# Low parts of weight tiles: two ScalarE copies and an adding DMA in place of a VectorE subtraction

## The chip, the core and the metric

The kernel runs on one core of a Trainium2 chip. The core has a tensor engine (TensorE, PE in the profile; its weight loads are PEld), a vector engine (VectorE, DVE), a scalar engine (ScalarE, ACT), GpSimd (POOL) and SyncE (SP). Each has a queue of its own and works it off in order; they meet through semaphores. DMA transfers are issued from a queue (SP's, or POOL's) and carried by 16 DMA engines that all queues share. The metric is the device time of one execution in microseconds.

## What is computed

One decoder layer on 1024 tokens of width 1024, all in float32. The reference, cut to what matters:

```python
for l in range(DEPTH):                                          # DEPTH = 1
    h = _layer_norm(ALPHA * h + 0.5 * _swiglu(h, ffn1...), ln1_g[l], ln1_b[l])
    mix = _token_mixers(h, w_in[l], lower_bounds[l], ..., w_out[l])
    h = _layer_norm(ALPHA * h + mix, ln2_g[l], ln2_b[l])
    xa = _memory_cross_attention(h, mem, mem_ln_g[l], mem_ln_b[l], xa_w_q[l], xa_w_k[l],
                                 xa_w_v[l], xa_w_o[l])
    h = _layer_norm(ALPHA * h + xa, ln3_g[l], ln3_b[l])
    h = _layer_norm(ALPHA * h + 0.5 * _swiglu(h, ffn2...), ln4_g[l], ln4_b[l])
```

The token mixers multiply h by `w_in` (1024 x 3072), whose column blocks feed a gated recurrence of four heads and a spatial gating unit; both outputs side by side are multiplied by `w_out` (1024 x 1024). The attention multiplies by `xa_w_q` and, at its end, by `xa_w_o` (1024 x 1024 each).

## The kernel before

Every product of two float32 matrices is made as three products in a shorter format (`F32R`): an operand is split into a high part, its value rounded to that format, and a low part, the rest. `mm3` (L130) then issues high x high, high x low and low x high (L131 to L133), all into the same PSUM bank.

Weights come in tiles of 128 partitions x 1024 values, 512 KB. `load_raw` (L112) issues the load on SP's queue (L118) into one of three buffers with the tag `raw`. `split_w` (L121) takes one of six `whi` and one of five `wlo` buffers and calls `split` (L108): ScalarE copies the raw tile into the high part (L109), VectorE subtracts the high part from the raw tile into the low part (L110). `load_split` (L127) is both. A raw buffer is free again when the low part has read it; high and low buffers are free again when TensorE has issued the last product that reads them.

The stages follow one another on TensorE: keys and values of the memory, the first FFN, the token mixers, the output projection, the attention, the second FFN. The FFNs have helpers of their own for their weights (`w_combos`, `down`), which call `split_w` directly. In the other stages weights are used in three ways:

- `feat_group` (L138), called by `feat_unit` (mixers: forget gate `wf`, query `wq`, gating input `wu`) and by `q_proj` (attention, `waq`): one tile holds all 1024 rows of 128 columns; 24 products with it make one bank.
- `token_units` (L779): four tiles hold 1024 rows of 512 columns and stay for four units, one per token tile, of 24 products each (values `wiv`, gating values `wvs`, output gate `wg`). They take four of the five low buffers as long as they are used.
- `down_group` (L226), for `w_out` (`wd_mx`) and `xa_w_o` (`wd_xa`): a group of two or three token tiles keeps two banks each; every step k loads one tile and issues 6 products with it per token tile. The groups are (0, 1), (2, 3, 4) and (5, 6, 7), and each loads all eight tiles anew.

The mixers go by halves of the tokens: values (`wiv`), gates and queries by head, gating inputs, gating values (`wvs`) of the first half; then the values and first gate of the second half; then the output gate (`wg`) of the first half; then the rest of the second half. The first group of `w_out` comes after the gating values of the second half, then the output gate of the second half, then the two groups of three. In the attention the products of the first group of `xa_w_o` lie between those of the heads.

What follows a product on other engines (recurrence, norms, gates) runs as coroutines: `tick` (L73) counts the time of issued products, and a coroutine yields how much of it should be issued before it goes on. `residual_norm` (L214) yields at least 6 us before its transposes. The norms use POOL for the reciprocal root, two instructions each (`rsqrt_eps`, L176; L179, L181, L182).

The program is issued in this order to a planner that simulates the engines and chooses each engine's final order from its own estimates of durations, so an instruction may move past others of its queue. POOL issues no DMA before the change. Six PSUM banks of 128 x 512 are shared by the products (`ps_mm`), two more by the transposes (`ps_tr`).

Of the kernel before, what the change touches and what calls it, by code (L numbers as in the profile page):

```python
# [8 lines left out]
F32 = mybir.dt.float32  # L9
F32R = mybir.dt.float32r  # L10
# [5 lines left out]
P = 128  # L16
# [17 lines left out]
def hybrid_layer_kernel(ctx: ExitStack, tc: tile.TileContext, a, out):  # L34
# [29 lines left out]
    # Work that follows a matrix product on other engines runs as a coroutine: where the tensor  # L64
    # engine would wait for it, it yields the time of other products (in us) to issue first.
# [26 lines left out]
    # the tensor engine's clock rises while it works: transposes until the first tile is there  # L92
# [9 lines left out]
    # left and right operands of the products of the FFNs' down projection, by pair of feature tiles  # L102
# [26 lines left out]

    def mm3(ps, lh, ll, rh, rl, first, last):  # L130
        nc.tensor.matmul(ps, lh, rh, start=first, stop=False)  # L131
        nc.tensor.matmul(ps, lh, rl, start=False, stop=False)  # L132
        nc.tensor.matmul(ps, ll, rh, start=False, stop=last)  # L133
# [11 lines left out]
    def to_xT(h_tile, tt, ks, name, keep=None):  # L145
        """Transpose the 128-column blocks of a token-major tile into xT's k-tiles ks; with keep,
        also as they are into tiles by (half of k, half of the tokens, pair of k-tiles)."""
        for _ in to_xT_steps(h_tile, tt, ks, name, keep):
            pass
# [57 lines left out]
    def layer_norm(y, gb, bb, name):  # L207
        """y: [P, 1024] tile, normalized over its free dim in place."""
# [5 lines left out]
    def residual_norm(tt, lag, acc, res_src, gb, bb, dst, name, keep=None):  # L214
        """dst = LN(alpha * res_src + acc) for a token tile, and its transpose."""
# [10 lines left out]
    def down_group(w, nk, grp, operand, res_src, gb, bb, dst, name, keep=None):  # L226
        """dst = LN(alpha * res_src + operand^T @ w) for the token tiles of grp; yields after each k."""
        acc = {tt: [ps_mm(f"acc_{name}_{tt}_{dh}") for dh in range(2)] for tt in grp}
        for k in range(nk):
            wh, wl = load_split(w[k * P:(k + 1) * P, :], f"wd_{name}_{grp[0]}_{k}")  # L230
# [21 lines left out]
    # Winograd's form of Strassen's product for W^T X^T with 2x2 blocks: rows are two feature  # L252
    # tiles, the contraction and the tokens are halved.
    def x_combos(xf, name):
        """Right operands of the products, in two stages."""
# [22 lines left out]
    def w_combos(w, f1, f2, name, pool=None):  # L278
        """Left operands of the products, in two stages: those of the first part, then all."""
# [19 lines left out]
    def strassen(wc, rhs, name):  # L299
        """Products of two feature tiles with all tokens, a tile each, in two parts: the first  # L300
        multiplies blocks of X as they are."""
# [26 lines left out]
    def ffn(wg, wu, wd, g, b, res_src, dst, make_xT, xf, name, start=None):  # L328
        """start: products that come before, given what to do late in them; without it, the first pair of
        feature tiles is multiplied without Strassen's form."""  # L330
# [70 lines left out]
    # The down projection h W has its blocks by half of the tokens, parity of the feature tile and  # L401
    # half of the columns.
    SLOT = {1: 0, 5: 1, 6: 2, 2: 3, 4: 4, 7: 5, 3: 6}

    def store_h(kp, h, tmp):
        """Left operands of the seven products for the feature tiles 2 kp and 2 kp + 1."""
# [10 lines left out]
    def down(wd, res_src, gb, bb, dst, make_xT, name):  # L417
# [5 lines left out]
        def right(ps, k, n):  # L423
            """Right operands: of two products for pair k, or of one for n pairs from k;
            combinations for later ones are kept."""
# [33 lines left out]
        # operands are made some steps ahead of their products  # L459
# [8 lines left out]
        # of product 3, the first operands take the place of xT, which has been used by then  # L468
# [22 lines left out]
        def pair(ps, when):  # L491
            """Two products, all tiles in step; returns their banks."""
# [20 lines left out]
        def single(p, done, hold):  # L513
            """One product; in its last steps, as many as hold says, its tiles end one after the other."""
# [36 lines left out]
        def norm(tt, wait):  # L551
# [3 lines left out]
            if tt < 4:  # L555
                # xT's place is free: what the scalar engine writes there is not used
# [222 lines left out]
    def token_units(half, c0, name, evac):  # L779
        """One unit per token tile of the half: x[tile] @ w_in[:, c0:c0+512], then evac(i, psum)."""  # L780
        wts = []

        def unit(i):
            if not wts:
                wts.extend(load_split(w_in[2 * j * P:(2 * j + 2) * P, c0:c0 + 512]
# [12 lines left out]
    def feat_unit(half, c, name, evac):  # L798
        """The feature tile c of x @ w_in for the half, transposed."""
        evac(feat_group(load_split(wcol(w_in, c), f"{name}{half}"), half, f"ps_{name}{half}"))  # L800

    class Mixers:
        """What the mixers keep of one half: v, o and u in pairs of tiles, and by head [k | q] and
        [b | log f, then scores]."""
# [80 lines left out]
        def recurrence(self, h):  # L885
            """Head h: gated scores within chunks of 128, states between the chunks, normed output."""
# [12 lines left out]
            def prep(j):  # L899
                """Levels 2j and 2j+1: k and q scaled by their decay to the border between their  # L900
                blocks; the last pair holds level 6 and k's decay to the end of its chunk."""
# [57 lines left out]
            # exp(b_end), exp(b) q  # L959
# [109 lines left out]
    qs, prs = {}, {}  # L1069

    def q_proj(half, c):
        wt = load_split(wcol(a["xa_w_q"][0], c), f"waq{half}_{c}")
# [134 lines left out]
```

## Time and profile before

| | us |
|---|---|
| median of 2 runs | 2037.99 |
| the two runs | 2035.06 and 2040.92 |
| span of the profiled execution | 2032.8 |

The span is the time from the first to the last instruction of one profiled execution; what lies around it is not in the profile. No other time of that execution is recorded, so the span is compared with the median of the runs, which is 5.2 us longer.

Where the stages lie in the span, by the first and the last product of each group on TensorE:

| stage | tile | from (us) | to (us) |
|---|---|---|---|
| mixers, values of both halves | `ps_wiv` | 704.5 | 877.6 |
| mixers, gating values of both halves | `ps_wvs` | 813.2 | 1019.9 |
| mixers, output gate of both halves | `ps_wg` | 893.3 | 1082.7 |
| output projection | `acc_mx` | 1022.2 | 1152.6 |
| attention, queries | `paq` | 1152.8 | 1265.6 |
| attention, output projection | `acc_xa` | 1275.2 | 1386.2 |

How to read the lines that follow: "L110 DVE ... x24 | 28.9, 1219 | 6.4 <-PE ..." is a group of instructions of line 110 on VectorE that ran 24 times, was busy 28.9 us in all and 1219 ns on average, and before which the engine had been idle for 6.4 us, ended by what stands behind the arrow. Names are those of the tiles: `_r` is a raw tile, `_h` a high part, `_l` a low part. A row of DMA issues ends with the KB of one transfer and the median time from its issue to its landing. In a table of stretches, a row has the stretch, its length, the busy time of each engine in it with the count of instructions, the clock that TensorE was granted, the busy share of the 16 DMA engines and the rate.

### The profile page before, as it was taken

The page shows a single profiled execution, that of the slowest core. Times are in us where ns is not written, and L with a number is a line of the kernel's source. Part 1 is how long each engine was busy: PE and PEld are TensorE (multiplying, and loading weights), DVE is VectorE, ACT ScalarE, POOL GpSimd, SP SyncE. Part 2 cuts the span into 40 slices and gives each one's busy share as a digit, 9 for nine tenths or more (in the row PEclk, how much of TensorE's full clock was granted, in tenths as well). Part 3 has the DMA queues.
Part 4 walks back from the last instruction along what each step waited for, and adds up shares of the span by engine and source line. Part 5 has one row for each costly group of instructions (what it writes and reads, how often), then busy time and mean ns, then how long its engine had stood idle before and what let it go on. Part 6 is the DMA issues. An engine that isn't in the chain of part 4 may idle for free.

```text
span 2032.8 us, 25339 instructions
## 1 busy us (share of the span) xinstructions
PE 2015.5 (99%) x9646; PEld 1689.1 (83%) x9646; DVE 1504.1 (74%) x2246; ACT 890.0 (44%) x1239; POOL 102.5 (5%) x144
## 2 busy tenths in 40 slices
PE   8999999999999999999999999999999999999998
PEld 7888888888888888888888888888888888888886
DVE  5987677677668967948796855678776776776688
ACT  6633333334533467547644344444333333344432
POOL 0000000000002010100110100010000000000021
PEclk8999999999999999999999999999999999999999
DMA  8333233237887632123156522353232332378874
GB/s 263 122 114 119 78 114 119 78 119 250 290 289 261 222 116 73 53 63 105 41 176 228 162 88 74 122 197 119 88 126 82 104 127 81 109 249 291 297 254 172
DMA packets 244250, 306.88 MB, mean 151 GB/s; under 512 B 14368, under 2 KB 154272, under 8 KB 244128
## 3 DMA queue, kind: packets, MB, share of 16 engines
q1 hardware_dynamic: 244128, 305.26, 45.3%
q8 instruction: 76, 1.25, 0.2%
q14 instruction: 46, 0.38, 0.1%
HBM read 234.44 MB, written 70.78 MB: 150 GB/s over the span
## 4 chain that ended last, share of the span: by engine, by line
PE 93%; DVE 3%; DMA 2%; POOL 1%; issue 1%; SPq 0%; ACT 0%; POOLq 0%; DVEq 0%; ACTq 0%
PE st_gf L131 7%; PE st_uf L131 7%; PE st_gf L133 7%; PE st_uf L133 7%; PE st_gf L132 7%; PE st_uf L132 7%; PE dp_f L133 6%; PE dp_f L131 6%; PE dp_f L132 6%; PE psl L939 2%; PE acc_xa L131 1%; PE acc_xa L133 1%; PE acc_xa L132 1%; PE paq L131 1%; PE paq L133 1%; PE paq L132 1%
## 5 line engine op out<-in xcount | busy, mean ns | idle before, releaser
L132 PE MATMUL dp_f<-wd_f_l,ah_f 128*128 128x512 f32 x552 | 213.3, 390 | 0.0
L131 PE MATMUL dp_f<-wd_f_h,ah_f 128*128 128x512 f32 x552 | 208.4, 390 | 0.0
L133 PE MATMUL dp_f<-wd_f_h,al_f 128*128 128x512 f32 x552 | 206.1, 390 | 0.1
L133 PEld LDWEIGHTS dp_f<-wd_f_h,al_f 128*128 128x128 f32 x552 | 103.7, 188 | 22.2 <-DVE al_f L110 0.9
L132 PEld LDWEIGHTS dp_f<-wd_f_l,ah_f 128*128 128x128 f32 x552 | 103.6, 188 | 21.6
L131 PEld LDWEIGHTS dp_f<-wd_f_h,ah_f 128*128 128x128 f32 x552 | 103.6, 188 | 21.2
L109 ACT ACTIVATE wd_f_h<-wd_f_r 128x1024 fp32r<-128x1024 f32 x72 | 73.2, 1022 | 97.7 <-DVE wd_f_r L436 28.3
L110 DVE TENSOR_TENSOR al_f<-ar_f,ah_f 128x1024 fp32r<-128x1024 f32 x72 | 84.5, 1174 | 24.5 <-ACT ah_f L109 23.6
L109 ACT ACTIVATE ah_f<-ar_f 128x1024 fp32r<-128x1024 f32 x72 | 73.3, 1019 | 59.2 <-DMA ar_f<-lops 54.3
L110 DVE TENSOR_TENSOR wd_f_l<-wd_f_r,wd_f_h 128x1024 fp32r<-128x1024 f32 x72 | 84.3, 1175 | 12.5 <-ACT wd_f_h L109 12.2
L316 DVE TENSOR_TENSOR top_uf<-bot_uf,st_uf 128x512 f32<-128x512 f32 x21 | 14.4, 686 | 81.8 <-PE st_uf L133 81.8
L315 ACT ACTIVATE bot_gf<-st_gf 128x512 f32<-128x512 f32 x21 | 12.5, 597 | 137.1 <-PE st_gf L133 137.1
L560 POOL TENSOR_SCALAR nm_f<-nm_f 128x1 f32<-128x1 f32 x8 | 10.7, 1336 | 1198.8 <-ACT xl L559 1198.8
L131 PE MATMUL st_gf<-xh,wg_f_h 128*128 128x512 f32 x168 | 65.4, 389 | 0.0
L133 PE MATMUL st_gf<-xh,wg_f_l 128*128 128x512 f32 x168 | 65.4, 389 | 0.0
L131 PE MATMUL st_uf<-xh,wu_f_h 128*128 128x512 f32 x168 | 65.4, 389 | 0.0
L132 PE MATMUL st_uf<-xl,wu_f_h 128*128 128x512 f32 x168 | 65.4, 389 | 0.0
L133 PE MATMUL st_uf<-xh,wu_f_l 128*128 128x512 f32 x168 | 65.4, 389 | 0.0
L132 PE MATMUL st_gf<-xl,wg_f_h 128*128 128x512 f32 x168 | 65.3, 389 | 0.0
L109 ACT ACTIVATE wg_f_h<-wg_f_r 128x1024 fp32r<-128x1024 f32 x44 | 46.4, 1056 | 36.2 <-PE st_gf L132 29.3
L109 ACT ACTIVATE wu_f_h<-wu_f_r 128x1024 fp32r<-128x1024 f32 x44 | 46.3, 1053 | 35.7 <-issue 27.2
L110 DVE TENSOR_TENSOR wu_f_l<-wu_f_r,wu_f_h 128x1024 fp32r<-128x1024 f32 x44 | 53.6, 1219 | 3.2 <-PE acc_xa L132 3.2
(456 smaller groups left out, 5960.1 us busy)
## 6 DMA issues: line engine op xcount, KB each, us to landing
ar_f<-lops SPq DMA_DIRECT2D x66, 512.0 KB, 5.0
wd_f_r<-in_ffn_w_down_dram SPq DMA_DIRECT2D x56, 512.0 KB, 4.8
wg_f_r<-in_ffn_w_gate_dram SPq DMA_DIRECT2D x44, 512.0 KB, 3.8
wu_f_r<-in_ffn_w_up_dram SPq DMA_DIRECT2D x44, 512.0 KB, 3.8
wd_mx_r<-in_w_out_dram SPq DMA_DIRECT2D x24, 512.0 KB, 3.6
wd_xa_r<-in_xa_w_o_dram SPq DMA_DIRECT2D x24, 512.0 KB, 3.5
lops<-bot_gf SPq DMA_DIRECT2D x21, 512.0 KB, 2.7
lops<-top_uf SPq DMA_DIRECT2D x21, 512.0 KB, 2.8
```

Source lines behind the costliest of these rows:

```text
L109: order(nc.scalar.activation(hi, src, AF.Copy))
L110: order(nc.vector.tensor_tensor(lo, src, hi.bitcast(F32), op=ALU.subtract))
L131: nc.tensor.matmul(ps, lh, rh, start=first, stop=False)
L132: nc.tensor.matmul(ps, lh, rl, start=False, stop=False)
L133: nc.tensor.matmul(ps, ll, rh, start=False, stop=last)
L315: nc.scalar.activation(b0, product(1), AF.Copy)
L316: nc.vector.tensor_tensor(t0, b0, product(2), op=ALU.add)
L560: nc.gpsimd.tensor_scalar(nmean, nmean, -1.0 / D, None, op0=ALU.mult)
L939: nc.tensor.matmul(psl[:m, (i * NC2 + c) * 64:(i * NC2 + c + 1) * 64] .rearrange("p (n b) -> p n b", b=B), e[:, :m], blk(e, B)[:, :, 1, :] ...
```

## The change

A new helper, `load_parts`, takes the place of `load_split` in `down_group`, `token_units`, `feat_unit` and `q_proj`. ScalarE writes the high part as before. It then writes the negated high part into the low buffer, and a DMA from POOL's queue adds the raw tile to it in SBUF. The helpers of the FFNs and the keys and values of the memory still use `split`. The comments taken out elsewhere change nothing.

```diff
+    def load_parts(view, name):
+
+        raw = load_raw(view, name)
+        hi = wpool.tile(list(raw.shape), F32R, tag="whi", bufs=6, name=f"{name}_h")
+        lo = wpool.tile(list(raw.shape), F32R, tag="wlo", bufs=5, name=f"{name}_l")
+        nc.scalar.activation(hi, raw, AF.Copy)
+        nc.scalar.activation(lo, hi.bitcast(F32), AF.Copy, scale=-1.0)
+        nc.gpsimd.dma_start(lo, raw, accum_op=ALU.add)
+        return hi, lo
...
         for k in range(nk):
-            wh, wl = load_split(w[k * P:(k + 1) * P, :], f"wd_{name}_{grp[0]}_{k}")
+            wh, wl = load_parts(w[k * P:(k + 1) * P, :], f"wd_{name}_{grp[0]}_{k}")
...
             if not wts:
-                wts.extend(load_split(w_in[2 * j * P:(2 * j + 2) * P, c0:c0 + 512]
+                wts.extend(load_parts(w_in[2 * j * P:(2 * j + 2) * P, c0:c0 + 512]
                                       .rearrange("(k p) c -> p k c", p=P), f"{name}{half}{j}")
                            for j in range(KT // 2))
...
-        evac(feat_group(load_split(wcol(w_in, c), f"{name}{half}"), half, f"ps_{name}{half}"))
+
+        evac(feat_group(load_parts(wcol(w_in, c), f"{name}{half}"), half, f"ps_{name}{half}"))
...
     def q_proj(half, c):
-        wt = load_split(wcol(a["xa_w_q"][0], c), f"waq{half}_{c}")
+        wt = load_parts(wcol(a["xa_w_q"][0], c), f"waq{half}_{c}")
```

## The prediction

> **What bounds the kernel now.** I read the page first: the busy shares, then the chain that ended last.
>
> ```profile
> span 2032.8 us, 25339 instructions
> ...
> PE 2015.5 (99%) x9646; PEld 1689.1 (83%) x9646; DVE 1504.1 (74%) x2246; ACT 890.0 (44%) x1239; POOL 102.5 (5%) x144
> ...
> q1 hardware_dynamic: 244128, 305.26, 45.3%
> ...
> PE 93%; DVE 3%; DMA 2%; POOL 1%; issue 1%; SPq 0%; ACT 0%; POOLq 0%; DVEq 0%; ACTq 0%
> ```
>
> TensorE is busy for 2015.5 of 2032.8 us, so at most 17.3 us of the span can be won by making any other engine faster. The next view is the table of stretches, to see where these 17.3 us lie (columns: PE, PEld, DVE, ACT, POOL busy with counts, clock, DMA share, GB/s).
>
> ```profile
> 0.00:60.00 60.00, 51.95 (x345) 48.06 (x346) 36.42 (x60) 36.55 (x79) 3.32 (x16) 0.91 0.90 277
> ...
> 740.00:800.00 60.00, 60.00 (x327) 50.97 (x325) 41.90 (x96) 44.91 (x54) 2.80 (x5) 1.00 0.27 82
> ...
> 1020.00:1060.00 40.00, 39.58 (x238) 34.32 (x236) 37.20 (x89) 19.35 (x27) 3.62 (x6) 1.00 0.57 196
> ...
> 1900.00:2033.00 133.00, 124.01 (x545) 101.62 (x543) 105.74 (x123) 45.34 (x54) 19.80 (x20) 0.98 0.67 230
> ```
>
> The start loses 8.05 us, the end 8.99 us; neither is touched. Of what is left, 0.42 us stands at 1020 to 1060, where VectorE is busy for 37.2 of 40 us. So the changed stages (mixers, output projection, attention) have half a microsecond to win. How fast TensorE eats weights, I take from the timeline:
>
> ```profile
> 1117.65 0.39 PE L132 MATMUL acc_mx<-wd_mx_l,xh 128*128 128x512 f32 x1
> ...
> 1119.92 0.39 PE L133 MATMUL acc_mx<-wd_mx_h,xl 128*128 128x512 f32 x1
> ```
>
> Ten products lie between these two starts, 0.227 us each (the 0.39 of one row overlaps its neighbours). A weight tile of 512 KB feeds 24 products in the mixers and the queries, 5.45 us; 18 in a group of three token tiles, 4.09 us; 12 in a group of two, 2.72 us.
>
> **The change, part by part.** VectorE loses one subtraction per tile.
>
> ```profile
> L110 DVE TENSOR_TENSOR wd_xa_l<-wd_xa_r,wd_xa_h 128x1024 fp32r<-128x1024 f32 x24 | 29.3, 1222 | 25.5 <-PE paq L133 16.9 <-PE acc_xa L132 7.8 <-issue 0.3
> L110 DVE TENSOR_TENSOR wd_mx_l<-wd_mx_r,wd_mx_h 128x1024 fp32r<-128x1024 f32 x24 | 28.9, 1219 | 6.4 <-PE acc_mx L132 4.2 <-issue 1.7 <-ACT wd_mx_h L109 0.2
> ...
> L110 DVE TENSOR_TENSOR waq_l<-waq_r,waq_h 128x1024 fp32r<-128x1024 f32 x16 | 19.6, 1224 | 27.8 <-PE paq L133 22.7 <-PE acc_mx L132 2.6 <-issue 2.5
> ...
> L110 DVE TENSOR_TENSOR wg_l<-wg_r,wg_h 128x1024 fp32r<-128x1024 f32 x8 | 9.8, 1224 | 6.6 <-ACT wg_h L109 3.2 <-PE ps_wf L133 3.0 <-PE ps_wiv L132 0.2
> ...
> L110 DVE TENSOR_TENSOR wiv_l<-wiv_r,wiv_h 128x1024 fp32r<-128x1024 f32 x8 | 9.6, 1218 | 0.0
> ```
>
> With 8 each of the six kinds from w_in (first and last shown) that is 24 + 24 + 16 + 48 = 112 tiles, 112 x 1.22 = 137 us of VectorE removed. TensorE did not wait for it: worth 0 to 0.4 us, I take 0.
>
> *ScalarE* gains one 128x1024 copy per tile, 112 x 1.06 = 119 us by the row of the high part:
>
> ```profile
> L109 ACT ACTIVATE wd_mx_h<-wd_mx_r 128x1024 fp32r<-128x1024 f32 x24 | 25.4, 1059 | 27.0 <-DMA wd_mx_r<-in_w_out_dram 12.2 <-PE acc_mx L133 10.7 <-PE ps_wvs L133 2.3
> ...
> DVE waq_l L110 <- PE paq L133: 22.7, 9, 4.1
> ```
>
> The tightest place is 740 to 800: 44.91 us busy, and TensorE can eat at most 60 / 5.45 = 11 tiles there, so ScalarE ends at 56.6 of 60. The cover is its remaining idle time; without it a bank's evacuation comes 1 to 4 us later. The wait for a free low-part buffer, until now VectorE's (up to 4.1 us), now stands in ScalarE's queue, with the evacuation of the products behind it. Six PSUM banks at 5.45 us a unit hide that: 0, and 2 x 1.06 us per unit at the worst if no bank were spare.
>
> *The accumulating DMA*, 112 of 512 KB, is the unknown; the trace has no DMA from POOL and none that adds. Call L its time from issue to landing. Nearest rows:
>
> ```profile
> wd_mx_r<-in_w_out_dram SPq DMA_DIRECT2D x24, 512.0 KB, 3.6
> ...
> lops<-bot_gf SPq DMA_DIRECT2D x21, 512.0 KB, 2.7
> ...
> kv<-kv SPq DMA_DIRECT2D x4, 512.0 KB, 6.8
> ...
> r_mx<-res SPq DMA_DIRECT2D x8, 512.0 KB, 8.4
> ```
>
> Lower bound: one plain transfer out of SBUF, 2.7 us. Upper: the slowest plain one and another after it, 8.4 + 2.7 = 11.1. I take 5.0 where the queues are quiet: 2.7, plus a second read of 512 KB at the rate of q1 (45.3% of 2032.8 us for 305.26 MB, 1.58 us), plus 0.7 for POOL's part, as its small instructions take (below). Where the queues are crowded, kv took 6.8 against 3.6; half of that surcharge makes L = 7, nearer to the quiet rows because these stretches are crowded only in part. The Trainium skill, page "DMA: Bandwidth & Descriptors", section "Anatomy of one DMA — SWDGE (gpsimd) path", gives about 2.0 us plus bytes over 436 GB/s for a plain DMA from this queue, 3.2 us here (an estimate from that page; no run here shows it); by it no term below is left and the time would be 2038.
>
> A tile's low part used to be ready 1.22 us after the high part; now after 1.06 + L and two hand-overs. What this can hold up is the buffers: three raw, six high, five low.
>
> ```profile
> SPq L118 <- DVE wd_mx_l L110: 98.9, 19, 28.2
> ...
> 1097.62 0.33 SPq L118 DMA_DIRECT2D wd_mx_r<-in_w_out_dram  x1
> ...
> 1096.36 1.23 DVE L110 TENSOR_TENSOR wd_mx_l<-wd_mx_r,wd_mx_h 128x1024 fp32r<-128x1024 f32 x1 [0.19 <-ACT wd_mx_h L109]
> ...
> L110 DVE TENSOR_TENSOR wd_mx_l<-wd_mx_r,wd_mx_h x24: 1171/1220/1234, 988.6 to 1131.6; 128x1024 fp32r<-128x1024 f32 x24
> ...
> L132 PE MATMUL acc_mx<-wd_mx_l,xh x128: 387/389/476, 1022.6 to 1152.4; 128*128 128x512 f32 x128
> ...
> L220 DVE SCALAR_TENSOR_TENSOR r_mx<-r_mx,acc_mx x16: 669/680/681, 1051.2 to 1155.2; 128x512 f32<-128x512 f32 x16
> ```
>
> Loads wait on SP until the low part has read a raw buffer. One turn of a raw buffer is issue 0.3, load 3.6, two copies 2.12, two hand-overs of 0.2, and L: 6.42 + L for three tiles. At L = 5 that is 3.8 us a tile (before: 2.1), below 5.45 and 4.09, so mixers, queries and groups of three keep their pace; they also have a lead, the last low part of w_out being done at 1133 and last used at 1152.
>
> Two places are short.
> - The seams, where a set of four column blocks (products of token tiles) ends and the next tiles follow at once: value-gate to wiv of the second half, value-gate to w_out. There a low buffer comes free 5.45 us before it is wanted, and 1.06 + 0.4 + 5.0 = 6.46 are needed: 1.0 us each, 2.0 together (0 at L = 2.7, 14 at 11.1).
> - The first group of w_out (two token tiles) with the gate's four tiles after it. The group runs from 1022.6 to 1051.2, with recurrences between, and all four gate tiles are wanted within 5.45 us after it: 12 tiles, three loaded beforehand, in 34 us. This stretch is crowded, so L = 7 and 4.47 us a tile: 9 x 4.47 = 40.2, 6 us late (0 at L = 2.7; 9 x 5.84 = 52.6, 18 late at 11.1). The same group of the attention runs between heads, with time to spare.
>
> *Queues that are passed.* On POOL the DMA waits for ScalarE's copy, and behind it stand the small steps of the norms:
>
> ```profile
> L179 POOL TENSOR_SCALAR ve_xa<-mv_xa 128x1 f32<-128x1 f32 x8 | 8.1, 1013 | 216.7 <-DVE mv_xa L196 216.7
> ...
> L182 POOL TENSOR_TENSOR rs_mx<-ve_mx,mhalf 128x1 f32<-128x1 f32 x8 | 6.4, 802 | 0.7
> ```
>
> VectorE waits for them, then the transposes. Their cover is the 6 us and more of products that the code puts before each transpose: 0; without it some 2 us for each of 16 norms. On SP, stores and residual loads stand behind a load that now waits longer; their users are covered in the same way.
>
> The sum: 2.0 + 6 = 8 us onto the profiled span, 2032.8 to about 2041. The median of the runs shown, 2037.99, is 5.2 us over that span; I keep this difference: 2046 us.
>
> **The rivals.**
>
> *Hidden altogether, 2037.* L near 3 and VectorE's relief at 1020 to 1060 pays its 0.4 us. For it: TensorE's idle time is nowhere in these stages. Against it: the raw buffers' turn grows in any case. This is also the time if the change works without doing anything for the clock.
>
> *The DMA engines become the bound in the output projection, 2072.*
>
> ```profile
> 1022.00:1051.00 29.00, 29.00 (x166) 24.75 (x165) 26.20 (x69) 13.27 (x15) 1.88 (x2) 1.00 0.60 205
> 1051.00:1087.00 36.00, 35.58 (x204) 30.80 (x203) 29.65 (x50) 16.73 (x35) 5.88 (x8) 1.00 0.34 120
> 1087.00:1120.00 33.00, 33.00 (x151) 27.38 (x150) 21.24 (x25) 15.08 (x17) 0.00 (x0) 1.00 0.80 294
> 1120.00:1152.00 32.00, 32.00 (x155) 26.66 (x154) 25.64 (x32) 10.69 (x13) 5.40 (x6) 1.00 0.54 170
> ```
>
> The shares make 73 us of engine time in 130. 28 tiles (24 of w_out, four gate) add 28 x 1.58 = 44 if an addition counts as one transfer, 117 in all, which fits; as two it adds 88, 162 in all, 32 us over, 34 with the seams. It decides from 2.0 us of engine time per tile. Against it: stores and key loads in that stretch can slip. A rule that speaks for it: the Trainium skill, page "Collectives: The Full Stack", section "The bandwidth ceiling: the fold count and why AG ≠ RS ≠ AR", says that an add in the DMA path needs two source reads in one ring and so runs at half the rate of a copy. No run here shows it yet.
>
> *Slower: the raw buffers' turn paces every stage, 2111.* At L = 11.1 a tile takes 5.84 us. Mixers and queries lose 64 x 0.39 = 25 us; the groups of three 32 x 1.75 = 56, less a lead of 20 us in each of two stages, 16; the first group 18; the seams 14: 73 in all. It passes 2% (41 us) at L of about 10. For it: 8.4 us for a plain residual load. Against it: most 512 KB rows lie at 2.7 to 5.
>
> *Faster:* no mechanism gives more than 0.4 us here.
>
> **How the numbers follow.** Forecast (2040 to 2060) 0.45; hidden 0.25; DMA-bound 0.12; paced by the raw buffers 0.16; something unseen 0.02. The likeliest gives 2046. The range takes in hidden and DMA-bound with room for a larger seam, 2034 to 2080, and leaves out 0.18. A measurement of this kernel tells a change from none at about 2%, that is below 1997 or above 2079. Faster 0.01; slower 0.16 plus a quarter of the DMA-bound case, 0.19; same 0.80.
>
> **What would show it.** Right: VectorE near 1367 us busy, ScalarE near 1009, TensorE idle only by some microseconds, and these at 1020 to 1060 and the seams; a landing time of the adding DMA of 4 to 7 us. Wrong upward: landing times of 10 us and more, and TensorE waiting for low parts in the groups of three. Wrong downward: landing near 3 us and SP no longer waiting. If TensorE waits for evacuations by ScalarE in the mixers, the cover that I gave ScalarE was not there.

## The result and the profile after

| | us |
|---|---|
| median before | 2037.99 |
| median after, 2 runs (2136.13 and 2140.02) | 2138.07 |
| ratio, with its 95% interval | 1.0481 [1.0423, 1.0539] |
| span of the profiled execution after (before: 2032.8) | 2134.4 |

The kernel became slower by 100 us, where 2046 was forecast with a range up to 2080. The page of the changed kernel:

```profile
span 2134.4 us, 25612 instructions
...
PE 2044.9 (96%) x9646; PEld 1703.8 (80%) x9646; DVE 1377.1 (65%) x2134; ACT 994.0 (47%) x1351; POOL 197.4 (9%) x256
...
q1 hardware_dynamic: 244128, 305.26, 42.8%
q0 software_dynamic: 16128, 58.73, 14.8%
...
PE 70%; DMA 15%; ACT 5%; issue 5%; DVE 4%; POOL 2%; SPq 0%; POOLq 0%; DVEq 0%; ACTq 0%
```

VectorE and ScalarE do what they were to do (1377 and 994 us busy), and the new queue q0 carries the additions. TensorE, with the same 9646 products, idles 89.5 us (span less busy) instead of 17.3, and is busy 29.4 us longer: 72.2 + 29.4 = 101.6, the whole growth of the span. The chain that ended last was 93% TensorE and is now 70%, with 15% DMA. What TensorE waits for, from the view of waits (total us, times, longest; the lines behind `load_split` have moved by 10):

```profile
PE pt_mx L168 <- DVE xl L110: 14.0, 3, 8.7
PE psl L949 <- ACT e L928: 11.0, 1, 11.0
PE acc_mx L142 <- DMA wd_mx_l<-wd_mx_r: 9.9, 6, 4.7
PE psl L949 <- DVE bs L952: 9.3, 3, 5.2
PE pt_xa L168 <- ACT xf_xa L182: 8.1, 1, 8.1
PE ps_wg L142 <- DMA wg_l<-wg_r: 5.7, 2, 3.3
PE acc_xa L142 <- DMA wd_xa_l<-wd_xa_r: 4.2, 1, 4.2
```

Only the three DMA rows, 19.8 us, are waits for low parts. The other four, 42.4 us, are few and long, and the work waited for has little to do with weights: transposes and exponentials. The longest of the first row is followed back in the chain of waits, in order of time (start, length, what):

```profile
1220.16 7.76 DMA waq_l<-waq_r
...
1227.98 5.72 DMA waq_r<-in_xa_w_q_dram
...
1235.16 1.05 ACT waq_l L136
...
1236.69 8.65 DMA waq_r<-in_xa_w_q_dram
...
1245.37 1.06 ACT waq_h L135
1246.42 0.49 ACT xh L109
...
1246.94 0.70 DVE xl L110
...
1247.68 1.11 PE pt_mx L168 x4
```

An addition lands at 1227.9 and only then frees a raw buffer for the next load. The load of 1236.69 lands late, at 1245.3. In ScalarE's queue the copy of that tile's high part stands in front of the evacuation `xh` of a transpose; the evacuation runs at 1246.4, and TensorE, which waits for its bank, has stood still for 8.7 us. ScalarE's own waits for raw loads show how often its queue stops so (waits of ScalarE; `waq_h` had 3.4 us of this before):

```profile
ACT waq_h L135 <- DMA waq_r<-in_xa_w_q_dram: 40.7, 13, 8.7
ACT wd_mx_h L135 <- DMA wd_mx_r<-in_w_out_dram: 38.9, 14, 6.7
ACT wd_xa_h L135 <- DMA wd_xa_r<-in_xa_w_o_dram: 36.3, 12, 8.0
```

The longer busy time goes with the granted clock, which falls in such stalls. Two stretches of 14 us, the first with this stall in it (columns: PE, PEld, DVE, ACT, POOL, clock, DMA share, GB/s):

```profile
1237.00:1251.00 14.00, 4.43 (x14) 3.54 (x15) 2.16 (x4) 4.54 (x7) 0.65 (x2) 0.53 0.83 237
1255.00:1269.00 14.00, 14.00 (x67) 11.69 (x66) 3.36 (x5) 7.36 (x10) 1.71 (x2) 1.00 0.64 151
```

And the landing times (last column, median us):

```profile
wd_mx_r<-in_w_out_dram SPq DMA_DIRECT2D x24, 512.0 KB, 5.7
wd_mx_l<-wd_mx_r POOLq DMA_DIRECT2D x24, 512.0 KB, 5.7
...
waq_r<-in_xa_w_q_dram SPq DMA_DIRECT2D x16, 512.0 KB, 5.4
waq_l<-waq_r POOLq DMA_DIRECT2D x16, 512.0 KB, 6.1
```

As a median the adding DMA takes 5.7 to 6.1 us in these rows, within the 4 to 7 that were forecast. The loads are slower than before as well: 5.7 us instead of 3.6 for `wd_mx_r`, 5.4 instead of 4.1 for `waq_r`.

### The profile page after: what moved, and what is told of

It reads as the page before. It is cut to its first block, busy times and chain, and to the rows that moved or that the text cites. A ratio compares the mean times of both kernels' runs of the same rounds, so it can differ in the third digit from the quotient of the medians.

```text
span 2134.4 us, 25612 instructions
## 1 busy us (share of the span) xinstructions
PE 2044.9 (96%) x9646; PEld 1703.8 (80%) x9646; DVE 1377.1 (65%) x2134; ACT 994.0 (47%) x1351; POOL 197.4 (9%) x256
## 3 DMA queue, kind: packets, MB, share of 16 engines
q0 software_dynamic: 16128, 58.73, 14.8%
## 4 chain that ended last, share of the span: by engine, by line
PE 70%; DMA 15%; ACT 5%; issue 5%; DVE 4%; POOL 2%; SPq 0%; POOLq 0%; DVEq 0%; ACTq 0%
PE st_gf L141 6%; PE st_gf L142 6%; PE st_uf L141 6%; PE st_uf L142 6%; PE st_uf L143 6%; PE st_gf L143 6%; PE dp_f L143 5%; PE dp_f L141 5%; PE dp_f L142 5%; DMA wd_mx_l<-wd_mx_r 2%; DMA waq_r<-in_xa_w_q_dram 2%; DMA wd_mx_r<-in_w_out_dram 1%; DMA wd_xa_r<-in_xa_w_o_dram 1%; PE acc_xa L141 1%; PE acc_xa L143 1%
## 5 line engine op out<-in xcount | busy, mean ns | idle before, releaser
L110 DVE TENSOR_TENSOR al_f<-ar_f,ah_f 128x1024 fp32r<-128x1024 f32 x72 | 84.3, 1172 | 22.3 <-ACT ah_f L109 22.1
L949 PE MATMUL psl<-e 128*128 128x64 f32 (+3 forms) x448 | 54.2, 269 | 23.9 <-ACT e L928 11.0
L949 PEld LDWEIGHTS psl<-e 128*128 128x128 f32 (+3 forms) x448 | 53.1, 188 | 29.6 <-ACT e L928 11.4
L325 ACT ACTIVATE bot_gf<-st_gf 128x512 f32<-128x512 f32 x21 | 12.5, 597 | 137.1 <-PE st_gf L143 137.1
```

What stands on the lines that cost most here:

```text
L110: order(nc.vector.tensor_tensor(lo, src, hi.bitcast(F32), op=ALU.subtract))
L325: nc.scalar.activation(b0, product(1), AF.Copy)
L949: nc.tensor.matmul(psl[:m, (i * NC2 + c) * 64:(i * NC2 + c + 1) * 64] .rearrange("p (n b) -> p n b", b=B), e[:, :m], blk(e, B)[:, :, 1, :] ...
```

## The experiments

Four theories, as the expectations name them. COPIES: ScalarE's 119 us more work delay the evacuations. LANDING: TensorE waits for the low parts themselves. HOLD: a raw buffer is held until the addition has landed, loads come late, and ScalarE's queue stops at them. DMA: the 16 DMA engines' own time sets the output projection of the mixers. Each run was timed beside the kernel before on the same chip. The last four columns are the lengthening of each stage in the profiled execution against before, from the first product of one stage to that of the next (the mixers are counted from the transposes `pw` of a small weight, at 723.2 us before; `acc_mx` begins the output projection of the mixers, `paq` the queries with what follows them, `acc_xa` that of the attention; lengths before: 299.0, 130.6, 122.4 and 111.2 us). The planner puts `pw` 3.4 us earlier in the changed kernel; counted from the first product of `ps_wiv`, its mixers lose 35.3 us instead of 38.6.

| kernel | median, us | ratio [95% interval] | mixers | proj. of mixers | queries | proj. of attention |
|---|---|---|---|---|---|---|
| changed | 2138.07 | 1.0481 [1.0423, 1.0539] | +38.6 | +25.2 | +18.0 | +21.7 |
| VectorE adds (e1) | 2038.14 | 0.9993 [0.9974, 1.0011] | -0.1 | -0.7 | -0.4 | +2.5 |
| VectorE negates (e2) | 2114.93 | 1.0359 [1.0335, 1.0383] | +19.0 | +25.8 | +14.2 | +22.3 |
| 4 raw (e4) | 2105.96 | 1.0317 [1.0294, 1.0340] | +13.6 | +23.7 | +7.8 | +13.4 |
| 5 raw, general pool 20 (e4) | 2184.93 | 1.0699 [1.0656, 1.0741] | +7.8 | +20.1 | 0.0 | +8.9 |
| 5 raw, 5 high (e13) | 2086.39 | 1.0235 [1.0208, 1.0263] | +5.9 | +21.7 | +2.8 | +7.8 |
| 6 low (e15) | 2107.63 | 1.0328 [1.0310, 1.0345] | +17.6 | +21.3 | +9.5 | +18.2 |
| 4 raw, 6 low, 5 high (e16) | 2096.82 | 1.0274 [1.0250, 1.0298] | +9.8 | +22.0 | +1.6 | +9.2 |
| adding DMA for w_out only (e5) | 2068.80 | 1.0144 [1.0119, 1.0168] | 0.0 | +28.2 | +2.4 | 0.0 |
| for all but w_out (e6) | 2107.49 | 1.0342 [1.0315, 1.0370] | +36.5 | +8.7 | +4.9 | +18.4 |
| 4 raw, half additions in w_out (e7) | 2090.71 | 1.0254 [1.0227, 1.0281] | +11.5 | +16.2 | +0.1 | +11.7 |
| one free store per tile (e12) | 2043.58 | 1.0016 [1.0000, 1.0032] | 0.0 | -0.6 | 0.0 | +1.3 |
| two free stores per tile (e12) | 2054.11 | 1.0072 [1.0050, 1.0094] | +10.5 | +0.5 | +4.2 | +5.0 |

Five more, told at the end, came out spoilt or beside the point.

**The copies alone, and the copy on VectorE.** First run: both copies stay on ScalarE, the addition goes to VectorE.

```diff
-        nc.gpsimd.dma_start(lo, raw, accum_op=ALU.add)
+        nc.vector.tensor_tensor(lo, raw, lo.bitcast(F32), op=ALU.add)
```

> The two copies on ScalarE stay (high part, negated high part: 112 x 1.06 us more than before), the adding DMA is replaced by an addition on VectorE. Theory HOLD (the raw buffer is held through the adding DMA, so loads come late, and ScalarE's queue stops at high-part copies that wait for them, with evacuations behind): a raw buffer's turn falls to about 7.8 us, 2.6 per tile, so 2038 to 2055 us and ScalarE's wait for raw loads back near 12 us per kind. Theory COPIES (119 us more work in ScalarE's queue alone delays the evacuations): still 2100 us or more. Theory LANDING (TensorE waits for low parts that land late, and loads are slowed by the additions' traffic): 2038 to 2045, as there is no such DMA.

Second run: the addition stays a DMA, the negated copy goes to VectorE.

```diff
-        nc.scalar.activation(lo, hi.bitcast(F32), AF.Copy, scale=-1.0)
+        nc.vector.tensor_scalar(lo, hi.bitcast(F32), -1.0, None, op0=ALU.mult)
```

> The negated copy moves from ScalarE to VectorE, the adding DMA stays: ScalarE has the work it had before the change. HOLD: the raw buffers are still held through 1.2 + 6 us and loads stay late, so most of the loss stays, 2090 to 2140; a little less if the negated copy no longer stands behind the next tile's load. COPIES: the loss goes, 2038 to 2050. LANDING: the loss stays, 2120 to 2140.

The first is as fast as before; the line of busy times on its page:

```profile
PE 2018.1 (99%) x9646; PEld 1689.9 (83%) x9646; DVE 1502.5 (74%) x2246; ACT 991.5 (49%) x1351; POOL 107.4 (5%) x144
```

ScalarE carries the added 101 us there (991.5 against 890.0) and TensorE does not notice. COPIES falls. The second keeps 74 of 100 us (2114.93 against 2040.49 for the kernel before in its run) with ScalarE back at its old load. The loss comes with the adding DMA. The other quarter, most of it in the mixers, is the place of the negated copy beside that DMA; what of the copy acts there was not isolated.

**More raw buffers.** A tag's count of buffers is changed, nothing else (for the second run also 20 instead of 22 general buffers, for the third five instead of six high ones, to make room).

```diff
-        raw = wpool.tile([P] + list(view.shape[1:]), F32, tag="raw", bufs=3, name=f"{name}_r")
+        raw = wpool.tile([P] + list(view.shape[1:]), F32, tag="raw", bufs=4, name=f"{name}_r")
```

> The changed kernel with four raw buffers for weights instead of three, nothing else. HOLD: a turn of the same length now serves four tiles, so most of the loss goes, 2045 to 2085, and ScalarE waits for raw loads at most half as long. COPIES: no change, 2120 to 2140. LANDING: landing times stay at 6 us, and the low parts come hardly earlier, 2110 to 2140.

> Five raw buffers, and to make room 20 instead of 22 buffers in the pool of general tiles. HOLD: below the kernel with four raw buffers, 2038 to 2060, unless the smaller general pool costs something of its own (then waits for general tiles show on VectorE and SP). COPIES and LANDING: 2110 to 2140.

> The changed kernel with five raw buffers, the general pool as it was, and five instead of six buffers for high parts. HOLD+DMA: mixers within 10 us of before, queries within 3, attention output within 8, output projection of the mixers 15 to 24 longer, FFN stages within 5: 2068 to 2090, below the 2106 of four raw buffers. If the fewer high buffers bind instead: TensorE or ScalarE waits for them and it is 2100 or more.

With three, four and five raw buffers the mixers lose 38.6, 13.6 and 5.9 us, the queries 18.0, 7.8 and 2.8, the projection of the attention 21.7, 13.4 and 7.8. This is HOLD, though four buffers gave less in all than it asked for (2105.96, outside its 2045 to 2085), and with five the second and the first FFN came out 9.6 and 5.9 us longer, where 5 was expected at most. The first FFN was 6.8 us longer in the profile with one free store too, which changes nothing in it, so a few microseconds there tell little. LANDING falls here: landing times grow with each buffer added (below), and the loss shrinks. The run with the smaller general pool missed its forecast for a reason of its own, in the FFN stages (waits of TensorE):

```profile
PE st_gf L141 <- ACT wg_f L109: 46.5, 19, 2.5
```

In the four changed stages it agrees with the third run. The projection of the mixers hardly answers: +25.2, +23.7, +21.7.

**Where the turn of a raw buffer is lost.** The loads of the queries' 16 tiles, first and last start (one row of the view of `waq_r`; before, then changed):

```profile
L118 SPq DMA_DIRECT2D waq_r<-in_xa_w_q_dram x16: 367/368/379, 1129.3 to 1200.5; - x16
```

```profile
L118 SPq DMA_DIRECT2D waq_r<-in_xa_w_q_dram x16: 367/368/379, 1199.0 to 1288.8; - x16
```

(1288.8 - 1199.0) / 15 = 5.99 us a tile, 18.0 for a turn of three buffers; the products use a tile in 5.45. But this mean joins two parts that differ. The first goes up to the tenth load (views of `waq_r` and `waq_l` in this stretch alone; the last row has the landing times of the seven additions):

```profile
L118 SPq DMA_DIRECT2D waq_r<-in_xa_w_q_dram x10: 367/368/379, 1199.0 to 1245.2; - x10
```

```profile
L137 POOL DMA_DIRECT2D waq_l<-waq_r x7: 852/875/943, 1207.1 to 1236.6; - x7
...
DMA to landing us min/median/max: 5.4/7.5/8.7
```

From one load to the next into the same buffer it is 16.0 us on average over the first seven tiles, 5.3 a tile: 5.8 for the load and 7.3 for the addition, where the prediction had 3.6 and 5, and only 0.25 between the two copies. The loss is made here: from the first product of the first tile to that of the eighth it takes 57.9 us instead of 40.8, from there to the last product 72.8 instead of 72.0. At 5.3 us a tile the loads are hardly faster than the products with their 5.45, and the lead is gone: the first load starts 14.2 us ahead of the first product, not 23.5, and this is no more than a load, two copies and an addition take. So the late load of the chain above reached TensorE at once.

In the second part a load starts every 7.3 us and 6.8 us pass between the two copies, as the low part's copy waits for a free low buffer. But TensorE does other products between those of the queries there and mostly takes 8 to 9 us from tile to tile, before the change too: these waits cost nothing.

The groups of three in the projection of the mixers are slower in the same way. The loads of the last group's eight tiles (before, then changed):

```profile
L118 SPq DMA_DIRECT2D wd_mx_r<-in_w_out_dram x8: 327/328/333, 1093.1 to 1121.1; - x8
```

```profile
L118 SPq DMA_DIRECT2D wd_mx_r<-in_w_out_dram x8: 327/328/328, 1158.5 to 1192.5; - x8
```

In the changed kernel the time from one of these loads to the next into the same buffer is 15.3 us on average (loads 6.0, additions 6.5, nothing between the copies): 5.1 a tile, where the products could use one in 4.09. The products of this group take 40.4 us instead of 35.2, and 8 x 5.1 is 41. With four and five raw buffers the loads and additions take longer, and the turn becomes 19.5 and 23.3 us, still 4.9 and 4.7 a tile. The two groups of three together take 69.4 us before, 82.2 in the changed kernel, 79.4 and 77.4 with four and five buffers, which fits how little the stage answers to them.

What the waits for a low buffer cost, of which there are five for six high parts, was tried by adding one. The view of `wvs_h` first for the changed kernel, then for one with a sixth low buffer:

```profile
L135 ACT ACTIVATE wvs_h<-wvs_r x8: 1039/1057/1061, 787.1 to 1005.6; 128x1024 fp32r<-128x1024 f32 x8
L136 ACT ACTIVATE wvs_l<-wvs_h x8: 1047/1052/1062, 797.3 to 1019.3; 128x1024 fp32r<-128x1024 f32 x8
```

```profile
L135 ACT ACTIVATE wvs_h<-wvs_r x8: 1041/1057/1058, 779.7 to 985.4; 128x1024 fp32r<-128x1024 f32 x8
L136 ACT ACTIVATE wvs_l<-wvs_h x8: 1048/1050/1064, 783.0 to 988.3; 128x1024 fp32r<-128x1024 f32 x8
```

The first low copy starts 10.2 us after the first high copy, and 3.3 with six. Over the 112 tiles, paired in order for each kind, the mean gap between the end of the high copy and the start of the negated copy is 3.99 us in the changed kernel and 0.54 with six low buffers. The edit of the last two runs of this kind is the count of low buffers (for the second of them also four raw buffers, and five high ones to make room):

```diff
-        lo = wpool.tile(list(raw.shape), F32R, tag="wlo", bufs=5, name=f"{name}_l")
+        lo = wpool.tile(list(raw.shape), F32R, tag="wlo", bufs=6, name=f"{name}_l")
```

> The changed kernel with six instead of five buffers for low parts. Theory LOW (the low buffers' turn holds up the output projection of the mixers): this stage falls from +25 to under +15 us, the others hardly move, 2110 to 2128. HOLD (the raw buffers set the pace, a free low buffer does not help): no stage moves by more than 5 us, 2130 to 2142.

> Four raw, six low and five high buffers, against five raw, five low and five high (2086) and four raw, five low and six high (2106). LOW: the output projection of the mixers falls from +22 to under +14 us, 2080 to 2098. HOLD: as with four raw buffers, 2100 to 2112, or above if five high buffers bind.

One low buffer takes a third of the loss back, from 1.0481 to 1.0328, more than either theory had allowed and not where they had put it: 21 us in the mixers and 8.5 in the queries, 4 in the projection of the mixers. The kernel with four raw, six low and five high buffers falls into LOW's range, but not for LOW's reason: it keeps its +22.0 in that projection. The loads of the queries with the sixth buffer:

```profile
L118 SPq DMA_DIRECT2D waq_r<-in_xa_w_q_dram x16: 367/368/384, 1174.9 to 1250.6; - x16
```

Over all 16 tiles that is 5.05 us a tile instead of 5.99, but the first seven turns take 15.0 us instead of 16.0, and TensorE still stalls there, for 6.0 us instead of 8.7. So how the sixth buffer acts is not settled: it ends the holding of raw buffers between the copies, and it also lets one more tile lie ready. The gap between the copies costs nothing by itself. Before the change it was 5.17 us on average between ScalarE's copy and VectorE's subtraction; with VectorE adding (e1) it was 4.83, with the negated copy in ScalarE's queue, and no time was lost.

**One stage alone, and all but one.** `load_parts` is kept for `w_out` only, then for all but `w_out`.

```diff
-            wh, wl = load_parts(w[k * P:(k + 1) * P, :], f"wd_{name}_{grp[0]}_{k}")
+            wh, wl = (load_parts if name == "mx" else load_split)(w[k * P:(k + 1) * P, :], f"wd_{name}_{grp[0]}_{k}")
```

> The adding DMA is used for the 24 tiles of w_out only; mixers, queries and attention output subtract on VectorE as before the change. From first product to last, the output projection of the mixers takes 130 us before, 154 in the changed kernel, and also 154 and 150 with four and five raw buffers. Theory HOLD+DMA (the raw buffers' turn sets mixers, queries and attention output, the 16 DMA engines' own time sets the output projection of the mixers): this stage stays 10 to 24 us longer and nothing else moves, 2048 to 2064. HOLD alone (the raw buffers everywhere): much the same time, but then the DMA share of this stage stays under 0.9. A loss that comes from the planner's other order as a whole: no sum over stages, any time between 2040 and 2138.

> The counterpart: all tiles but those of w_out take the adding DMA. HOLD+DMA and HOLD: the other three stages keep their loss (39 in the mixers, 18 in the queries, 22 in the attention output) and the output projection of the mixers goes back to 130 to 136 us, 2105 to 2122 in all, and with the kernel before the losses of the two partial kernels add to about 100 us. The planner's order as a whole: no sum.

31.3 us against the before of its run, and 70.0: together 101.3, against 100.1 for the whole change. In the first, the mixers and the projection of the attention, left as they were, keep their lengths; a new order of the whole program is not the main cause. But both expectations missed in part. The first time lies above its 2064, with +28.2 in its stage where 24 was the most, at a DMA share of 0.85 (135 us of engine time in 158.7): the sign that had been named for HOLD alone. In the second the queries lose 4.9 us where 18 was expected, and the projection, back on VectorE, 8.7 where it was 6 at most. So the sum comes out partly by luck: by stages the two runs give 36.9 against 25.2 for the projection and 7.3 against 18.0 for the queries. This fits a lead that is lost in one stage and missing in the next, which no run isolates.

**The DMA engines.** In the projection of the mixers half the columns of each tile are taken from the DMA (with four raw buffers):

```diff
+        n = 512 if name.startswith("wd_mx") else 0
+        if n:
+            nc.vector.tensor_tensor(lo[:, n:], raw[:, n:], hi[:, n:].bitcast(F32), op=ALU.subtract)
+            nc.scalar.activation(lo[:, :n], hi[:, :n].bitcast(F32), AF.Copy, scale=-1.0)
+            nc.gpsimd.dma_start(lo[:, :n], raw[:, :n], accum_op=ALU.add)
+            return hi, lo
```

> Four raw buffers, and for the tiles of w_out the DMA adds the first 512 columns only, while VectorE subtracts the others: half the adding traffic in this stage, against the kernel with four raw buffers and whole tiles (2106 us, this stage 154). HOLD+DMA: 24 tiles x 1.4 us = 34 us of DMA engine time go, the stage falls to 131 to 142 us, 2083 to 2096 in all. HOLD alone: by (6.4 + 8.2) / 4 = 3.7 us a tile the four buffers had already been enough, so the stage was held up by something else and stays at 150 to 154, 2100 to 2106.

The total is in the range, the stage is not: it goes from +23.7 to +16.2, 7.5 us of the 12 or more that DMA asked for. It holds 0.84 x 146.8 = 123 us of engine time, less than the 130.6 of the stage before, and is still longer. So the traffic was put alone: VectorE subtracts as before, and POOL issues one or two plain stores of the high part that nobody waits for.

```diff
-        nc.scalar.activation(hi, raw, AF.Copy)
-        nc.scalar.activation(lo, hi.bitcast(F32), AF.Copy, scale=-1.0)
-        nc.gpsimd.dma_start(lo, raw, accum_op=ALU.add)
+        split(raw, hi, lo)
+        for i in range(2):
+            nc.gpsimd.dma_start(dram.tile([P, 1024], F32, name=f"{name}_s{i}"),
+                                hi.bitcast(F32).rearrange("p a b -> p (a b)") if len(hi.shape) == 3 else hi.bitcast(F32))
```

> VectorE subtracts as before the change; POOL issues for each of the 112 tiles one plain store of the high part, 512 KB, into DRAM that nobody reads and that waits for nothing but the high part. By the share of q1 a plain 512 KB takes some 1.6 us of engine time, an adding one 2.8. DMA: the output projection of the mixers needs 73 + 28 x 1.6 = 118 us of engine time, which fits into its 130: 2038 to 2046. HOLD alone: the same. If any work on POOL's queue costs time: the waits for the norms grow and 2060 or more comes out.

> The same with two stores for each tile, 3.2 us of engine time, somewhat more than one adding DMA. DMA: 73 + 28 x 3.2 = 163 us of engine time for the output projection of the mixers; it becomes 12 to 30 us longer, the other stages 0 to 8 each: 2052 to 2085. HOLD alone: 2038 to 2046, since nothing waits for these transfers and no raw buffer is held.

Two stores take as much of the engines as one addition took (page of this kernel, queue q0; the changed kernel has 14.8%):

```profile
q0 software_dynamic: 32256, 117.45, 14.9%
```

The projection of the mixers in the changed kernel, then with the two stores:

```profile
1057.40:1213.20 155.80, 137.38 (x672) 112.14 (x670) 68.72 (x139) 77.84 (x100) 32.23 (x42) 0.97 0.93 243
```

```profile
1032.60:1163.70 131.10, 130.49 (x671) 109.84 (x671) 97.68 (x168) 50.79 (x72) 39.82 (x66) 1.00 0.97 376
```

With the DMA engines at 0.97 TensorE still runs through: +0.5 us, where DMA had 12 to 30. Engine time by itself does not make this stage long. It would set a floor where transfers can't slip: the changed kernel puts 0.93 x 155.8 = 145 us of engine time into this stage, more than its 130.6 us of products, while with the stores 0.97 x 131.1 = 127 us are done there and the rest slips into the queries. But the run with half the additions lies below such a floor and loses 16.2 us all the same. What more traffic does show is slower landings. With three raw buffers the additions of this stage land in 5.7 us (median, above); the rows of DMA issues have

```profile
wd_mx_l<-wd_mx_r POOLq DMA_DIRECT2D x24, 512.0 KB, 8.0
```

with four, and

```profile
wd_mx_l<-wd_mx_r POOLq DMA_DIRECT2D x24, 512.0 KB, 9.6
```

with five: more transfers under way, none of them sooner. Over all stages the traffic of two stores costs 2054.1 - 2038.2 = 16 us, where the change costs 100 (the +10.5 of the mixers is more than the 8 that was allowed to any other stage); one store per tile costs 5, hardly clear of the noise and within its forecast. Of the 25 us of this stage the groups of three make up 12.8 in the changed kernel. How its loss divides between the turn of the raw buffers, a floor of engine time and residual tiles that load late is not settled.

**Spoilt or beside the point.** An addition into one tile that nobody reads (`dma_start(junk, hi, accum_op=ALU.add)`) was to be the traffic alone:

> VectorE subtracts as before the change, so raw buffers come free early; beside it POOL issues for each of the 112 tiles an adding DMA of the high part into a tile that nobody reads. Only the traffic of the change is there, no wait for it. DMA (the 16 DMA engines' time sets the output projection of the mixers): this stage is 10 to 20 us longer than 130, the other stages within 3 us of before each, 2048 to 2062. HOLD alone: 2037 to 2042 in all stages, since no raw buffer is held longer.

2132.45 us, 1.0462 [1.0447, 1.0478], outside every forecast: the additions into the same tile waited for each other on POOL's queue, with the norms behind them. Waits of VectorE there (11.5 us in the kernel before):

```profile
DVE ot L1028 <- POOL hrs L194: 59.0, 6, 14.4
```

It says nothing of the traffic, but it shows that POOL's queue has no such cover as was given to it. In the changed kernel this wait is 25.0 us.

The negated copy on POOL (`nc.gpsimd.tensor_scalar(lo, hi.bitcast(F32), -1.0, None, op0=ALU.mult)`), with three and four raw buffers, and both copies on POOL:

> The negated copy moves to POOL, whose queue then issues the DMA. In the changed kernel the negated copy starts on average 4.0 us after the high part's copy has ended, by other work in ScalarE's queue; here that falls below 1 us, and POOL's copy may take 1 to 3 us. HOLD: a raw buffer's turn, 18.5 us before, falls to 15 to 17, 5.1 to 5.8 us per tile, near the 5.45 of mixers and queries: these two lose 10 to 25 us instead of 57, the other two stages stay, 2085 to 2110. If the delay in the queue doesn't matter: 2125 to 2140.

> The same with four raw buffers: 15 to 17 us over four is 3.8 to 4.3 a tile. HOLD+DMA: mixers and queries within 5 us of before, attention output within 8, only the output projection of the mixers keeps its 15 to 24 us, 2058 to 2078. HOLD alone: 2040 to 2050.

> High part and negated copy both on POOL, three raw buffers: neither ScalarE nor VectorE ever waits for a raw load of these tiles, so no evacuation or exponential stands behind one. Theory BLOCK (late loads cost time above all since ScalarE's queue stops at them, with evacuations behind): TensorE's waits for ScalarE vanish and the loss in mixers and queries falls to under 20 us, 2060 to 2090. HOLD by late operands (TensorE would wait for the weights anyway): the waits move to high and low parts, 2095 to 2140.

2180.47 us, 1.0705 [1.0688, 1.0721]; 2125.67, 1.0424 [1.0406, 1.0441]; 2255.56, 1.1065 [1.1049, 1.1082]. All three missed. POOL's copy takes nearly three times ScalarE's 1.06 us and holds the raw buffer all the while; whether this is the whole reason was not isolated:

```profile
L136 POOL TENSOR_SCALAR wd_mx_l<-wd_mx_h 128x1024 fp32r<-128x1024 f32 x24 | 68.6, 2882 | 71.5 <-ACT wd_mx_h L135 62.9 <-PE acc_mx L142 8.4
```

With both copies there TensorE waits for low parts instead of ScalarE; how much of the loss goes through ScalarE's stopped queue could not be told apart in this way.

The addition reading the weights again from DRAM, so that the raw buffer is free after the first copy (`dma_start(lo[:, sl], view[:, sl], accum_op=ALU.add)`, in four parts for tiles of feature columns):

> The adding DMA reads the weights again from DRAM and not from the raw buffer, which is free after the high part's copy; tiles of feature columns take four smaller DMAs. Three raw buffers, landing times not shorter than before. HOLD+DMA: mixers, queries and attention output come back to within 5 us each of before (299, 113 and 111 us), the output projection of the mixers stays long or grows, since the traffic stays: 2050 to 2085. LANDING (TensorE waits for the low parts themselves, whenever the raw buffers come free): 2110 or more. POOL's issues, three more for each of 64 tiles, could cost something of their own (0.9 us each on POOL); then waits for the norms show.

2514.97 us, 1.2330 [1.2300, 1.2361]. The mixers lose 269 us and the queries 136, both with column tiles, whose low parts TensorE now waits for. Only the two projections, with one addition per tile of theirs, are comparable: that of the attention loses 12.5 instead of 21.7, with landings of 8.6 us, that of the mixers 37.8 instead of 25.2, with landings of 9.6.

No version beat the kernel before. TensorE is busy there for all but 17 us.

## Why the prediction was wrong, by its steps

- *VectorE's relief is worth nothing*: right. VectorE has 127 us less and no stage is faster.
- *ScalarE's 119 us are hidden*: right for the work (101 us measured; with VectorE adding, 0.9993). Wrong for the queue: "Six PSUM banks at 5.45 us a unit hide that: 0" counted one short wait. What came were stops of up to 8.7 us at late loads in the rows above, with evacuations behind them; that TensorE would wait for these was named as the sign of a missing cover.
- *L of 5 to 7*: right as a median, 5.7 to 6.1 in the rows above. But the value for quiet queues, 5.0, was put into the turn, and where tiles ran out it was 6.5 to 7.3.
- *The turn of a raw buffer, "6.42 + L for three tiles ... so mixers, queries and groups of three keep their pace"*: this is the step that failed. It put the load at 3.6 us and L at 5, and got 11.4 us, 3.8 a tile. Where TensorE ran out of tiles, loads took 5.8 to 6.0 us and additions 6.5 to 7.3, and the turn was 15.3 to 16.0 us, 5.1 to 5.3 a tile. In the groups of three that is above 4.09, and they lost 12.8 us where 0 was forecast; with the prediction's own L of 7 the sum would have given 4.47, above 4.09 as well. In the queries 5.3 against 5.45 leaves no room for a late load. The lead was gone as well: the last low part of `w_out` landed 4 us before its last use, not 19. For the mixers the cause is shown by the count of raw buffers (38.6, 13.6 and 5.9 us), not by a turn measured tile by tile. The sum also left out the time for which a raw buffer is held for want of a low one; a sixth low buffer brought back a third of the loss, and how it acts is open.
- *The rival that the raw buffers pace every stage, 2111*: its mechanism is what happened in three stages. Its threshold, L of about 10, came from the same short turn, with loads of 3.6 us; at an L of 6 to 7 and loads of 6 the loss was already 4.8%.
- *The seams and the first group, 8 us, at L of 7*: the stage lost 25, and waits for low parts are there (9.9 us, longest 4.7). The first group and the stretch up to the next, with the gate's tiles, lost 11.3 us where 6 were forecast; the rest is above all in the groups of three.
- *The DMA-bound rival, 2072*: its price per addition was nearly right, 14.8% of 2134.4 us for 112 tiles is 2.82 us of engine time where 3.16 was taken (twice 1.58). That engine time decides by itself from 2.0 us on is wrong: two stores with the same time cost that stage 0.5 us, and 16 in all.
- *POOL's and SP's queues, 0*: not quite. VectorE waits 25.0 instead of 11.5 us for the norms of the heads; what this costs TensorE wasn't isolated.
- *The granted clock* had no term; TensorE is busy 29 of the 102 us longer, and that much at most goes with it.

## What to carry to other kernels

Where a slow step is put into a chain that holds a buffer, add up the whole time from the issue of one load to the next into that buffer, the waits for other buffers included, and compare it with the time in which the consumer uses a tile. Take the times for it from the busiest stretch, not from quiet rows: here a load of 3.6 us became 6, and an addition put at 5 took up to 7.3 on average. And count the lead: a step that takes as long as the lead leaves none for a late load. In an in-order queue a late load does not delay its own tile alone, but everything behind it, and that may be what the busiest engine waits for.

## What the runs showed of the hardware

An adding DMA of 512 KB within SBUF takes 2.82 us of engine time, a plain store of the same size 1.37 (14.9% of 2055.8 us for 224): a ratio of 2.06. The Trainium skill, page "Collectives: The Full Stack", section "The bandwidth ceiling: the fold count and why AG ≠ RS ≠ AR", gives half the rate for the adding step of a collective, since it reads two sources. These runs agree in size, though they set an addition within SBUF against a store to DRAM.

After the stall of 8.7 us the products of 512 columns start 0.43 us apart instead of 0.227 (view of TensorE's instructions in order of time):

```profile
1249.02 0.63 PE L143 MATMUL paq<-xh,waq_l 128*128 128x512 f32 x1
1249.45 0.63 PE L141 MATMUL paq<-xh,waq_h 128*128 128x512 f32 x1
1249.88 0.63 PE L142 MATMUL paq<-xl,waq_h 128*128 128x512 f32 x1
```

The Trainium skill, page "TensorE: Matmul & The Clock Gate", section "Part 1: The HAM clock gate", says that the array falls to half its clock after an idle window of about 3.4 us and needs as long a busy one to rise again. The trace agrees in kind: the stretch with the stall above was granted 0.53 of the clock. At most 29 of the 102 us are this, the growth of TensorE's busy time, on top of the stalls themselves.
